# Layer 2's token tiles, normalised and turned inside layer 1's attention

## The chip, the cores and the metric

The kernel runs on one core of a Trainium2 chip. The metric is the device time of one execution in microseconds (us). Names of engines as in the profile: PE is TensorE's matmul, PEld its weight load, DVE is VectorE, ACT is ScalarE, POOL is GpSimd, SP is SyncE, which issues most DMAs.

## What is computed

The reference is a backbone of two layers over 1024 latent tokens and 256 context tokens of width 1024, all in float32. Each layer adds a gated mixer of a normalised input to its tokens:

```python
for i in range(DEPTH):
    ...
    hx = rms_norm(x, norm_g[i]) * (1.0 + scale_x[:, None]) + shift_x[:, None]
    hc = rms_norm(ctx, norm_g[i]) * (1.0 + scale_c) + shift_c
    if kind == 0:
        yx, yc = window_gqa(hx, hc, a_w_in[j], a_sink[j], a_w_out[j], cos_a, sin_a, need_ctx)
    elif kind == 1:
        yx, yc = latent_attention(hx, hc, b_w_in[j], b_q_norm[j], b_w_uq[j], b_kv_norm[j],
                                  b_w_ukv[j], b_w_out[j], cos_b, sin_b, need_ctx)
    ...
    x = x + gate_x[:, None] * yx
```

Layer 1 is a windowed attention with grouped heads and a sink, layer 2 an attention over a latent projection (kv of 256 columns and 32 rotary ones, q of 512, a gate of 1024). The change stands where one layer hands its tokens to the next: rms_norm and the affine map with scale and shift, which give h, and the first projections of h.

## The kernel before

The tokens are ten tiles of 128: tiles 0 and 1 are context, 2 to 9 latent. Two tiles are a pair; h is kept by pairs. All matmuls of the projections are made of three: each operand is split into a rounded part and a rest (`split`: a cast on ACT, L121, and a subtraction on DVE or POOL, L122), and `mm3` issues the three products (L126 to L128).

The order of the work is that in which the program issues it, rearranged by a scheduler within each engine; every engine then runs its own list in order and waits on others by semaphores. On-chip memory is two arenas, F (float32) and R (rounded halves), in which buffers are named by an offset in KB per partition; a `Ring` hands out buffers in turn, and what is written over earlier contents waits until these have been read.

*Layer 1's attention* walks over 40 units: ten tiles in the order 2, 0, 3, 1, 4 to 9, with four groups of heads each. A unit scores four heads (L586) and takes the minimum and the mask on DVE (L597), the exponential on ACT (L600), turns the probabilities by chunks of 128 keys (L617, then the cast L121 and the subtraction L122) and multiplies them with V (L627). The steps of neighbouring units are interleaved: a unit's scores are issued two units ahead, its gate (`g_d`) two, its q three. At a unit's end `fin` copies the product (L637) and adds its halves (L639); `fin2`, one unit later, turns the reciprocal sums, copies them (L648), and makes the gated output. After the fourth group of a tile its output projection is handed out in pieces among the next tile's units (`outproj`, L657 to 676): the tile's x is loaded (L658), the product with the gate vector is taken on DVE (L674), added (L675), and the result is stored to the DRAM buffer `x1_d` (L676).

*The start of layer 2* loads each tile back from `x1_d` (`norm_x`, L212), takes its sum of squares on ACT (L214), the mean and the power of -1/2 (L215 on DVE, L216 on POOL), scales the tile on DVE (L217), turns it with eight transposes in two banks (`turn_x`, L224), and copies them (L225) into the turned pair of `[8, 256]`. `build_h` then applies scale and shift by eighths (L238 on DVE), casts (L241 on ACT) and subtracts (L243, here on DVE). Pairs 0 and 1 are made ahead of the last pieces of the last output projection, pairs 2 to 4 inside the loop over the ten kv tiles. A kv tile is 24 matmuls of 288 columns (`kv_tile`); its statistic (L958 to 960) scales it (L997 on DVE), and two tiles later its turn stands on PE (L1010). The weights of layer 2 come through a ring of staging buffers `stg`: loaded by L264, cast on ACT and subtracted on DVE (the kv block) or POOL (the others). The vector q_norm is loaded by ACT's queue (L972) to F at 8 KB, where layer 1's gate vector `gx` lay, and multiplied on DVE (L973).

## Time and profile before

| | before |
|---|---|
| median of three runs | 1597.75 us (1595.53, 1597.75, 1597.89) |
| the profiled execution | 1596.15 us |
| its span, first to last instruction | 1594.4 us |
| mean granted TensorE clock | 0.997 of full speed |
| PE, PEld busy | 98%, 77% |
| DVE, ACT, POOL busy | 57%, 49%, 47% |
| DMA | 192.82 MB, mean 121 GB/s |

The profile is one execution. A row of a group names line, engine and operation, what it writes and reads, and how often; then busy time, the mean of one in ns, the idle time of the engine just ahead of it, and what ended that. A row of a timeline gives start and length in us; brackets hold the idle time ahead. A stretch is start and end in us. An engine's idle time costs nothing where another engine sets the pace.

### The profile page before, as it was taken

The page shows a single profiled execution, that of the slowest core. Times are in us where ns is not written, and L with a number is a line of the kernel's source. Part 1 is how long each engine was busy: PE and PEld are TensorE (multiplying, and loading weights), DVE is VectorE, ACT ScalarE, POOL GpSimd, SP SyncE. Part 2 cuts the span into 40 slices and gives each one's busy share as a digit, 9 for nine tenths or more (in the row PEclk, how much of TensorE's full clock was granted, in tenths as well). Part 3 has the DMA queues.
Part 4 walks back from the last instruction along what each step waited for, and adds up shares of the span by engine and source line. Part 5 has one row for each costly group of instructions (what it writes and reads, how often), then busy time and mean ns, then how long its engine had stood idle before and what let it go on. Part 6 is the DMA issues. An engine that isn't in the chain of part 4 may idle for free.

```text
span 1594.4 us, 26916 instructions
## 1 busy us (share of the span) xinstructions
PE 1555.2 (98%) x9938; PEld 1222.6 (77%) x9938; DVE 905.9 (57%) x1629; ACT 777.0 (49%) x1478; POOL 742.1 (47%) x805
## 2 busy tenths in 40 slices
PE   7899999999999999998999999999999999999998
PEld 4787777887878888887998899766766766766687
DVE  3515551618777777768525302667677677667454
ACT  3522232348777777767523332455545555555322
POOL 1231112115664444454113350388688688689510
PEclk9999999999999999999999999999999999999999
DMA  7446776354333333327113753313232233244251
GB/s 253 166 138 196 233 210 190 97 153 120 109 110 94 97 93 94 93 79 244 35 34 106 262 184 94 103 30 101 69 96 80 76 88 96 67 130 118 67 167 66
DMA packets 147203, 192.82 MB, mean 121 GB/s; under 512 B 13936, under 2 KB 84080, under 8 KB 147072
## 3 DMA queue, kind: packets, MB, share of 16 engines
q1 hardware_dynamic: 145456, 188.94, 39.5%
q10 hardware_dynamic: 1616, 2.17, 0.5%
q8 instruction: 78, 1.28, 0.4%
q14 instruction: 53, 0.43, 0.1%
HBM read 144.90 MB, written 46.15 MB: 120 GB/s over the span
## 4 chain that ended last, share of the span: by engine, by line
PE 86%; issue 2%; DVE 2%; POOL 2%; ACT 2%; DMA 1%; SPq 0%; POOLq 0%; DVEq 0%; ACTq 0%
PE PB L126 15%; PE PB L127 14%; PE PB L128 14%; PE PB L1303 11%; PE PB L1325 8%; PE PB L586 5%; PE PB L627 4%; PE PB L1266 4%; PE PB L617 4%; PE PB L183 1%; PE PB L1274 1%; PE PB L1354 1%; PE PB L646 1%; ACT arena_r L121 1%; DVE arena_r L122 1%
## 5 line engine op out<-in xcount | busy, mean ns | idle before, releaser
L126 PE MATMUL PB<-arena_r 128*128 128x512 f32 (+3 forms) x1496 | 509.9, 342 | 4.9 <-POOL arena_r L653 2.0
L127 PE MATMUL PB<-arena_r 128*128 128x512 f32 (+3 forms) x1496 | 502.4, 336 | 4.2 <-DVE arena_r L390 2.1
L128 PE MATMUL PB<-arena_r 128*128 128x512 f32 (+3 forms) x1496 | 500.3, 335 | 0.3 <-DVE arena_r L122 0.3
L1317 POOL TENSOR_TENSOR arena_f<-arena_f 128x512 f32<-128x512 f32 x252 | 328.3, 1303 | 82.1 <-ACT arena_f L1309 65.3
L126 PEld LDWEIGHTS PB<-arena_r 128*128 128x128 f32 x1496 | 283.7, 190 | 52.7 <-issue 12.5
L127 PEld LDWEIGHTS PB<-arena_r 128*128 128x128 f32 x1496 | 284.5, 190 | 32.0 <-DVE arena_r L390 3.5
L128 PEld LDWEIGHTS PB<-arena_r 128*128 128x128 f32 x1496 | 284.5, 190 | 28.3 <-DVE arena_r L122 0.5
L122 POOL TENSOR_TENSOR arena_r<-arena_f,arena_r 128x512 fp32r<-128x512 f32 x88 | 115.2, 1325 | 299.7 <-ACT arena_r L121 255.5
L1309 ACT ACTIVATE arena_f<-PB 128x1024 f32<-128x1024 f32 x160 | 164.1, 1027 | 108.9 <-PE PB L1303 65.9
L1268 DVE TENSOR_REDUCE arena_f<-PB 128x1 f32<-128x1024 f32 x128 | 156.1, 1219 | 86.7 <-PE PB L1266 86.6
L1303 PE MATMUL PB<-arena_r 64*128 64x512 f32 (+1 forms) x1600 | 202.3, 392 | 0.3 <-ACT arena_f L1309 0.3
L1303 PEld LDWEIGHTS PB<-arena_r 64*128 64x128 f32 (+1 forms) x1600 | 146.1, 185 | 31.5 <-ACT arena_f L1309 1.8
L122 DVE TENSOR_TENSOR arena_r<-PB,arena_r 128x512 fp32r<-128x512 f32 (+1 forms) x186 | 124.2, 674 | 61.9 <-ACT arena_r L121 61.0
L1325 PE MATMUL PB<-arena_f 128*64 128x512 f32 x640 | 144.4, 597 | 0.0
L600 ACT ACTIVATE arena_f<-arena_f,small 128x640 f32<-128x640 f32 (+2 forms) x160 | 119.5, 747 | 35.4 <-DVE small L597 32.7
L597 DVE CUSTOM_DVE_ANT_0 arena_f<-PB,arena_f,small 128x640 f32<-128x640 f32 (+2 forms) x176 | 125.2, 722 | 20.1 <-PE PB L586 12.6
L121 ACT CAST arena_r<-PB 128x512 fp32r<-128x512 f32 (+1 forms) x186 | 105.3, 573 | 47.4 <-PE PB L617 45.2
L121 ACT CAST arena_r<-arena_f 128x512 fp32r<-128x512 f32 (+3 forms) x141 | 83.8, 603 | 86.7 <-PE PB L128 12.5
L627 PE MATMUL PB<-arena_r 128*128 128x512 f32 x336 | 115.8, 429 | 0.5 <-DVE arena_f L639 0.5
L586 PE MATMUL PB<-arena_r 128*128 128x256 f32 (+1 forms) x576 | 111.0, 308 | 1.6 <-DVE small L597 1.3
L1325 PEld LDWEIGHTS PB<-arena_f 128*64 128x64 f32 x640 | 43.1, 136 | 83.2 <-issue 79.9
L617 PE MATMUL PB<-ident,arena_f 128*128 128x128 f32 x672 | 104.2, 274 | 1.3 <-DVE arena_r L122 0.8
(177 smaller groups left out, 1842.9 us busy)
## 6 DMA issues: line engine op xcount, KB each, us to landing
arena_f<-ada_w SPq DMA_DIRECT2D x47, 512.0 KB, 5.4
arena_r<-q_d SPq DMA_DIRECT2D x80, 256.0 KB, 3.9
arena_r<-qn_d SPq DMA_DIRECT2D x64, 256.0 KB, 3.9
arena_r<-qr_d SPq DMA_DIRECT2D x192, 64.0 KB, 3.3
arena_f<-a_w_in SPq DMA_DIRECT2D x40, 256.0 KB, 3.6
arena_f<-x SPq DMA_DIRECT2D x16, 512.0 KB, 6.6
g_d<-arena_f SPq DMA_DIRECT2D x32, 256.0 KB, 2.1
q_d<-arena_f SPq DMA_DIRECT2D x64, 128.0 KB, 2.4
```

What stands on the lines that cost most here:

```text
L121: nc.scalar.copy(hi, src)
L122: (lo_eng or nc.vector).tensor_sub(lo, src, hi.bitcast(F32))
L126: nc.tensor.matmul(o, ah, bh, start=first, stop=False)
L127: nc.tensor.matmul(o, al, bh, start=False, stop=False)
L128: nc.tensor.matmul(o, ah, bl, start=False, stop=last)
L586: nc.tensor.matmul(S[:, at : at + n], qT[:, s, hq, :], kT[:, g, k : k + n], start=s == 0, stop=s == 1)
L617: nc.tensor.transpose(pt[:, h, :], self.Ps[h][:, ci * 128 : ci * 128 + 128], ident)
L627: nc.tensor.matmul(self.pv, V[:, self.chunks[ci], self.g, :], PT[:, s], start=ci == 0 and s == 0, stop=ci == self.m - 1 and s == 1,)
L1303: nc.tensor.matmul(S[:, t], k[r, c : c + 128], q[r], start=j == 0, stop=j == 4)
L1309: nc.scalar.activation(E, self.S, AF.Exp)
L1317: eng.tensor_add(self.acc, self.acc, E[:, t])
L1325: nc.tensor.matmul(self.pv[p : p + 64], Vq[:, cs[t], self.h % 4, :], E[:, t], start=i == 0, stop=i == 4)
```

## The change

`norm_x` is parted into the load and `scale_x`. A DRAM buffer `xT_d` holds four turned pairs. The generator `pre_turns` does, for tiles 0 to 7: load the tile from `x1_d` into the one buffer `xpre`; scale it (L219 to 222: the lines of `scale_x` in the changed kernel); turn one half of it into a bank of the attention's own two (L689), copy that on ACT (L690) into the one buffer `tpre`, and store it to `xT_d` (L692); the same for the other half. These four steps are called at the ends of the attention's units, from tile position 5 on, two for each unit (one at position 8). At unit 38 pair 0 is loaded from `xT_d`, two halves of 256 KB.

Layer 2 loads pairs 1, 2 and 3 (`load_xt`) in place of `build_x`; `build_h` works on two half buffers. h(2) and h(3) are built at kv tiles 0 and 2. Tiles 8 and 9 are normalised and turned in layer 2 as before, and h(4) is built at kv tile 5. The buffers of F are laid out anew: `or1`, `rtr`, `gr`, `junk`, `stg` (three of 512 words for three of 576), `xr` (two for three), the last three of `qst`; `xtr` goes. The instructions on PE, DVE, ACT and POOL are as many as before; SP issues 24 DMAs more.

```diff
@@ -74,6 +74,7 @@
     q0_d = dpool.tile([4, 64, 2, NT, 512], F32, name="q0_d")
     g0_d = dpool.tile([8, 128, TOK], F32, name="g0_d")
     x1_d = dpool.tile([TOK, D], F32, name="x1_d")
+    xT_d = dpool.tile([4, 128, 8, 256], F32, name="xT_d")
     qn_d = dpool.tile([8, 128, 2, SEQ], F32, name="qn_d")
     qr_d = dpool.tile([4, 128, 2, SEQ], F32, name="qr_d")
     g1_d = dpool.tile([8, 128, SEQ], F32, name="g1_d")
@@ -210,37 +211,35 @@
     def norm_x(src, xr, junk):
         x = xr.next()
         load(out=x, in_=src)
+        scale_x(x, junk)
+        return x
+
+    def scale_x(x, junk):
         st = sm_ring()
         nc.scalar.activation(junk, x, AF.Square, accum_out=st[:, 0:1])
         nc.vector.tensor_scalar(st[:, 1:2], st[:, 0:1], 1.0 / D, EPS, ALU.mult, ALU.add)
         nc.gpsimd.tensor_tensor(st[:, 2:3], st[:, 1:2], mhalf, ALU.pow)
         nc.vector.tensor_scalar_mul(x, x, st[:, 2:3])
-        return x
 
     def turn_x(x, xt, j):
         for q in range(2):
             ps = shp(pst(), 4, 128)
             for c in range(4):
                 nc.tensor.transpose(ps[:, c, :], x[:, (4 * q + c) * 128 : (4 * q + c + 1) * 128], ident)
-            nc.scalar.copy(xt[:, 4 * q : 4 * q + 4, j * 128 : j * 128 + 128], ps)
-
-    def build_x(p, src, xr, xtr, junk):
-
-        xt = shp(xtr.next(), 8, 256)
-        for j in range(2):
-            turn_x(norm_x(src(2 * p + j), xr, junk), xt, j)
-        return xt
+            nc.scalar.copy(xt[q][:, :, j * 128 : j * 128 + 128], ps)
 
     def build_h(p, xt, hT, A, B, fast=False, ks=range(8)):
 
         w = 1 if p == 0 else 0
         for k in ks:
-            nc.vector.tensor_scalar(xt[:, k, :], xt[:, k, :], A[:, k, w : w + 1], B[:, k, w : w + 1], ALU.mult, ALU.add)
+            x = xt[k // 4][:, k % 4, :]
+            nc.vector.tensor_scalar(x, x, A[:, k, w : w + 1], B[:, k, w : w + 1], ALU.mult, ALU.add)
             if k % 2:
+                x = xt[k // 4][:, k % 4 - 1 : k % 4 + 1, :]
                 hi = hT[:, 0, k - 1 : k + 1, :]
-                nc.scalar.copy(hi, xt[:, k - 1 : k + 1, :])
+                nc.scalar.copy(hi, x)
                 eng = nc.vector if fast or k % 4 == 1 else nc.gpsimd
-                eng.tensor_sub(hT[:, 1, k - 1 : k + 1, :], xt[:, k - 1 : k + 1, :], hi.bitcast(F32))
+                eng.tensor_sub(hT[:, 1, k - 1 : k + 1, :], x, hi.bitcast(F32))
 
     class SmallRing:
         def __init__(self, n, w):
@@ -515,9 +514,9 @@
     ytmp = Ring(F, [12], 512)
     wstg = Ring(F, [4, 6, 12], 512)
     rbr = Ring(F, [42, 47], 256)
-    or1, rtr = (Ring(F, [o, o - 5], 256) for o in (43, 45))
+    or1, rtr = Ring(F, [43, 44], 256), Ring(F, [45, 41], 256)
     Pr = Ring(F, [14 + 2.5 * i for i in range(8)], 640)
-    gr = Ring(F, [2.5, 34, 46], 256)
+    gr = Ring(F, [34, 35, 46], 256)
     xr0 = Ring(F, [4], 1024)
     Wo = [r_at(o, 2, 1024) for o in (16, 24, 32, 40, 48, 56, 0, 8)]
     ogr = Ring(R, [64, 72], 2048)
@@ -676,6 +675,34 @@
         load(out=x1_d[ti * 128 : ti * 128 + 128, :], in_=x)
 
     units = [UnitA(ti, g) for ti in ORDER for g in range(4)]
+    xpre, tpre = f_at(48, 1024), f_at(36, 4, 128)
+
+    def pre_turn(ti):
+        load(out=xpre, in_=x1_d[ti * 128 : ti * 128 + 128, :])
+        yield
+        scale_x(xpre, f_at(36, 512).bitcast(BF16))
+        yield
+        for q in range(2):
+            ps = shp(pst3(), 4, 128)
+            for c in range(4):
+                k = 4 * q + c
+                nc.tensor.transpose(ps[:, c, :], xpre[:, k * 128 : k * 128 + 128], ident)
+            nc.scalar.copy(tpre, ps)
+            ts = slice(ti % 2 * 128, ti % 2 * 128 + 128)
+            load(out=xT_d[ti // 2, :, 4 * q : 4 * q + 4, ts], in_=tpre)
+            yield
+
+    def pre_turns():
+        for ti in range(8):
+            yield from pre_turn(ti)
+
+    xt_at = [[f_at(o, 4, 256) for o in os] for os in ((48, 36), (14, 18), (22, 26), (14, 18), (22, 26))]
+
+    def load_xt(p):
+        for q in range(2):
+            load(out=xt_at[p][q], in_=xT_d[p, :, 4 * q : 4 * q + 4, :])
+
+    pre = pre_turns()
 
 
     def wo_load():
@@ -910,6 +937,10 @@
             while i > 0 and done < -(-8 * i // steps):
                 next(filler, None)
                 done += 1
+        for _ in range({5: 2, 6: 2, 7: 2, 8: 1, 9: 2}.get(ui // 4, 0)):
+            next(pre, None)
+        if ui == 38:
+            load_xt(0)
         u.fin(og)
         fins.append(u.fin2)
         if u.g == 3:
@@ -930,10 +961,9 @@
     sinb = f_at(1, 8, 32)
     qn = f_at(8, 512)
     kvn = f_at(10, 256)
-    junk = f_at(34.5, 512).bitcast(BF16)
-    stg = Ring(F, [30, 32.25, 49.5], 576)
-    xr = Ring(F, [22, 26, 45], 1024)
-    xtr = Ring(F, [14, 37], 2048)
+    junk = f_at(40, 512).bitcast(BF16)
+    stg = Ring(F, [30, 32, 44], 512)
+    xr = Ring(F, [48, 36], 1024)
     ev = Ring(F, [2, 4, 6, 12], 512)
     ukK = r_at(134, 2, 2, 1024)
     ukV = r_at(64, 2, 2, 1024)
@@ -961,10 +991,10 @@
         return st[:, 2:3]
 
     fetch1(0, nc.vector)
-    xts = {0: build_x(0, src1, xr, xtr, junk)}
-    build_h(0, xts.pop(0), hT1[0], ada1.A, ada1.B, fast=True)
-    xts[1] = build_x(1, src1, xr, xtr, junk)
-    build_h(1, xts.pop(1), hT1[1], ada1.A, ada1.B, fast=True)
+    load_xt(1)
+    build_h(0, xt_at[0], hT1[0], ada1.A, ada1.B, fast=True)
+    load_xt(2)
+    build_h(1, xt_at[1], hT1[1], ada1.A, ada1.B, fast=True)
     load2(out=cosb, in_=t["cos_b"].rearrange("p (t d) -> p t d", t=8))
     load2(out=sinb, in_=t["sin_b"].rearrange("p (t d) -> p t d", t=8))
     for _ in last_outproj:
@@ -1097,17 +1127,17 @@
         ch = (c0 - 800) // 128
         load(out=g1_d[ch : ch + 2, :, (p - 1) * 256 : p * 256].rearrange("c p n -> p c n"), in_=shp(gg, 2, 256))
 
-    nx = norm_x(src1(4), xr, junk)
+    load_xt(3)
+    nx = {8: norm_x(src1(8), xr, junk)}
     for ti in range(NT):
-        n = ti + 3
-        if 4 <= n < NT:
-            if n % 2 == 0:
-                xt = shp(xtr.next(), 8, 256)
-            turn_x(nx, xt, n % 2)
-            if n + 1 < NT:
-                nx = norm_x(src1(n + 1), xr, junk)
-            if n % 2:
-                build_h(n // 2, xt, hT1[n // 2], ada1.A, ada1.B, fast=True)
+        if ti in (0, 2):
+            build_h(ti // 2 + 2, xt_at[ti // 2 + 2], hT1[ti // 2 + 2], ada1.A, ada1.B, fast=True)
+        if ti == 1:
+            nx[9] = norm_x(src1(9), xr, junk)
+        if ti in (4, 5):
+            turn_x(nx[ti + 4], xt_at[4], ti % 2)
+        if ti == 5:
+            build_h(4, xt_at[4], hT1[4], ada1.A, ada1.B, fast=True)
         kv_tile(ti)
         flush(2)
         if ti > 1 and ti % 2:
@@ -1119,7 +1149,7 @@
     fetch1(3, nc.vector)
     fetch1(4)
     rtmp = Ring(F, [14, 28], 512)
-    qst = Ring(F, [16, 20, 24, 37, 41, 45], 1024)
+    qst = Ring(F, [16, 20, 24, 36, 48, 8], 1024)
     for ti in range(8):
         qr_tile(ti)
         flush(2)
```

On ACT, around the first pre-turned tile in the attention (position 5 of ten). L600, L637, L648 and L121 of before are L599, L636, L647 and L122 of the changed kernel. Before:

```order
L637 COPY arena_f<-PB 64x256 x2
L121 CAST arena_r<-PB 128x512
L600 ACTIVATE arena_f,small<-arena_f,small 128x640
L648 COPY arena_f<-PB 128x256
L121 CAST arena_r<-PB 128x512
L600 ACTIVATE arena_f,small<-arena_f,small 128x640 x2
L121 CAST arena_r<-PB 128x512
```

and now:

```order
L636 COPY arena_f<-PB 64x256 x2
L690 COPY arena_f<-PB 128x512
L599 ACTIVATE arena_f,small<-arena_f,small 128x640
L647 COPY arena_f<-PB 128x256
L122 CAST arena_r<-PB 128x512
L599 ACTIVATE arena_f,small<-arena_f,small 128x640 x2
L690 COPY arena_f<-PB 128x512
L122 CAST arena_r<-PB 128x512
```

The two copies of the tile's halves (L690) have come in among the unit's exponentials and casts; the second stands five instructions behind the first, and of the casts that stood between the copies of the product (L637) and the third exponential one stands later now.

On DVE, from the last product of the last output projection to the first scaled kv tile. In before L674 and L675 are the product and the addition, L217 scales a tile of x, L238 and L243 build h, L973 scales q_norm, L959 belongs to kv's statistic and L997 is the scaled kv tile:

```order
L674 TENSOR_TENSOR arena_f<-PB,arena_f 128x512
L217 TENSOR_SCALAR arena_f<-arena_f,small 128x1024
L238 TENSOR_SCALAR arena_f<-arena_f,small 128x256 x6
L243 TENSOR_TENSOR arena_r<-arena_f,arena_r 128x512 x3
L238 TENSOR_SCALAR arena_f<-arena_f,small 128x256 x2
L675 TENSOR_TENSOR arena_f<-arena_f 128x512
L973 TENSOR_SCALAR arena_f<-arena_f 128x512
L959 TENSOR_SCALAR small<-small 128x1
L243 TENSOR_TENSOR arena_r<-arena_f,arena_r 128x512
L997 SCALAR_TENSOR_TENSOR arena_f<-PB,small,arena_f 128x256
```

and now (L673, L674, L236, L242, L1003, L989 and L1027 are the same steps):

```order
L673 TENSOR_TENSOR arena_f<-PB,arena_f 128x512
L1003 TENSOR_SCALAR arena_f<-arena_f 128x512
L674 TENSOR_TENSOR arena_f<-arena_f 128x512
L236 TENSOR_SCALAR arena_f<-arena_f,small 128x256 x5
L242 TENSOR_TENSOR arena_r<-arena_f,arena_r 128x512 x3
L236 TENSOR_SCALAR arena_f<-arena_f,small 128x256 x2
L989 TENSOR_SCALAR small<-small 128x1
L236 TENSOR_SCALAR arena_f<-arena_f,small 128x256
L1027 SCALAR_TENSOR_TENSOR arena_f<-PB,small,arena_f 128x256
```

The scaling of q_norm stood behind the building of a pair and stands now directly behind the last product; the pair built there is pair 1 in before and pair 2 now. On PE the first kv turn (L1010 in before, L1040 now) stands behind 75 matmuls of 288 columns.

## The prediction

> **What bounds the kernel now.** I read the page first, then the table of stretches, then what TensorE waited for at the end of the first attention. The page's busy line and the head of its chain:
>
> ```profile
> PE 1555.2 (98%) x9938; PEld 1222.6 (77%) x9938; DVE 905.9 (57%) x1629; ACT 777.0 (49%) x1478; POOL 742.1 (47%) x805
> PE 86%; issue 2%; DVE 2%; POOL 2%; ACT 2%; DMA 1%; SPq 0%; POOLq 0%; DVEq 0%; ACTq 0%
> ```
>
> TensorE is busy for 98% of the span and is most of the chain, so an edit pays only where TensorE idles or runs at a lower clock. The stretches (start:end, length, then busy time of PE, PEld, DVE, ACT, POOL, then the granted clock, the DMA share and GB/s) tell the attention apart from the start of layer 2:
>
> ```profile
> 480.00:700.00 220.00, 219.40 (x1318) 188.57 (x1317) 168.01 (x341) 161.44 (x378) 111.92 (x193) 1.00 0.32 94
> 720.00:762.00 42.00, 34.24 (x224) 30.60 (x223) 36.25 (x79) 30.96 (x66) 18.73 (x21) 0.96 0.69 212
> 750.00:754.00 4.00, 4.00 (x35) 4.00 (x33) 3.51 (x4) 1.91 (x5) 4.00 (x5) 1.00 0.54 150
> 754.00:758.00 4.00, 0.91 (x8) 0.71 (x6) 4.00 (x9) 2.97 (x6) 0.99 (x1) 0.96 0.64 180
> 758.00:762.00 4.00, 3.77 (x21) 3.78 (x22) 3.66 (x12) 3.04 (x9) 1.62 (x3) 0.61 0.00 0
> ```
>
> The attention (480 to 700 us) is full: 0.6 us of 220 idle. ACT and DVE are at 73% and 76% there, POOL at 51%. The start of layer 2 (720 to 762) has 42.00 - 34.24 = 7.8 us of idle TensorE, and its clock falls behind the longest hole: 4 x 0.04 + 4 x 0.39 = 1.7 us lost in the last two stretches. Together 9.5 us: that is all the change can win. The waits behind it, from 700 to 860 us (line <- releaser: us, times, longest):
>
> ```profile
> PE PB L1010 <- ACT arena_f L225: 3.3, 1, 3.3
> PE PB L224 <- DVE small L959: 1.2, 1, 1.2
> PE PB L126 <- ACT arena_r L241: 1.1, 1, 1.1
> PE PB L224 <- DVE arena_f L217: 0.9, 1, 0.9
> PE PB L127 <- DVE arena_r L243: 0.6, 1, 0.6
> PE PB L224 <- DVE small L215: 0.5, 1, 0.5
> PE PB L128 <- DVE arena_r L122: 0.3, 1, 0.3
> PE PB L627 <- DVE arena_f L639: 0.2, 1, 0.2
> ```
>
> Three waits of the turns (L224, 2.6 us) and two for the halves of h (1.7 us) belong directly to the step that is moved. The largest, 3.3 us at L1010, turns a kv result; what it has to wait for is everything queued on DVE and ACT ahead of that result.
>
> **The change part by part.** *The turns.* These are the rows of what eight of ten tiles move (the counts are those of ten tiles):
>
> ```profile
> L224 PE MATMUL PB<-ident,arena_f 128*128 128x128 f32 x80 | 11.2, 276 | 2.8 <-DVE small L959 1.2 <-DVE arena_f L217 0.9 <-DVE small L215 0.5
> L225 ACT COPY arena_f<-PB 128x512 f32<-128x512 f32 x20 | 11.2, 585 | 2.4 <-PE PB L224 2.4
> L214 ACT ACTIVATE arena_f<-arena_f 128x1024 bf16<-128x1024 f32 x10 | 10.6, 1059 | 0.7 <-DMA arena_f<-x_d 0.5
> L214 ACT ACTIVATION_READ_ACCUMULATOR arena_f<-arena_f 128x1 f32 x10 | 1.9, 190 | 0.0
> L217 DVE TENSOR_SCALAR arena_f<-arena_f,small 128x1024 f32<-128x1024 f32 x10 | 7.5, 753 | 4.5 <-POOL small L216 4.4
> L216 POOL TENSOR_TENSOR small<-small 128x1 f32<-128x1 f32 x10 | 6.0, 602 | 10.1 <-DVE small L215 9.2 <-DVE small L959 0.8
> ```
>
> On TensorE the 64 transposes cost the same in both places. Eight of them take from one start to the next matmul:
>
> ```profile
> 748.52 1.09 PE L224 MATMUL PB<-ident,arena_f 128*128 128x128 f32 x8 [1.24 <-DVE small L959]
> 749.36 0.38 PE L126 MATMUL PB<-arena_r 128*128 128x288 f32 x1
> ```
>
> 0.84 us, so 8 x 0.84 = 6.7 us leave layer 2 and 6.7 us come into an attention that has no hole for them: net nothing. What counts is idle time alone.
>
> *What the attention pays.* ACT gets 8 x (1.059 + 0.190 + 2 x 0.585) = 19 us, DVE 8 x 0.753 = 6 us plus small ones, POOL 8 x 0.602 = 5 us. In the 180 us in which they fall, ACT and DVE have idle a quarter of the time (some 48 and 43 us), so there is room on average. The cost is order: every engine works in order, and a copy that waits holds the casts behind it, for which P x V on TensorE waits. The one new wait of that kind is the single buffer of the turned half: the second copy (L690 after) waits until the store of the first half has been read out. Between the two copies ACT has one exp, one copy of 128x256, one cast and two exps, by these rows (from 500 to 600 us; L617 are the attention's own turns that the cast follows):
>
> ```profile
> L600 ACT ACTIVATE arena_f<-arena_f,small 128x640 f32<-128x640 f32 x40 | 33.4, 834 | 7.9 <-DVE small L597 6.9
> L121 ACT CAST arena_r<-PB 128x512 fp32r<-128x512 f32 x49 | 28.5, 586 | 18.4 <-PE PB L617 18.1
> L617 PE MATMUL PB<-ident,arena_f 128*128 128x128 f32 x200 | 29.6, 272 | 0.0
> L648 ACT COPY arena_f<-PB 128x256 f32<-128x256 f32 x10 | 3.6, 356 | 0.0
> g_d<-arena_f SPq DMA_DIRECT2D x32, 256.0 KB, 2.1
> x_d<-arena_f SPq DMA_DIRECT2D x6, 512.0 KB, 2.7
> arena_f<-x SPq DMA_DIRECT2D x5, 512.0 KB, 3.5
> ```
>
> Cover: 3 x 0.834 + 0.356 + 0.586 = 3.4 us. The store moves 256 KB; the nearest row is g_d's 2.1 us, a 512 KB store takes 2.7. With some 0.4 us until SP has issued it, the round trip is 2.5 to 3.1 us: under the cover, with 0.3 to 0.9 us in hand. If a 512 KB load is ahead of it in the DMA queue (3.5 us), the round trip is up to about 4.7 and ACT stands 1.3 us. The 1.25 us Square and the two copies also delay a cast by up to their own length, against the idle of 18.1 us in 49 casts that ACT has in waiting for L617, 0.37 us each. So per tile 0 to 0.75 us of TensorE, all in 0 to 6 us; not below nothing by more than the 0.6 us that the stretch idles now. I take 1.7 us, 0.2 for each tile, since the row that is nearest (the g_d store) leaves the cover standing and no TensorE wait over 0.2 us stands in this stretch now. What SP issues more (8 loads and 16 stores, and loads of the turned pairs for two of x1) goes at nothing: loads of q and g are issued three and two units ahead, and the DMA share is 0.32. If a store waits on SP for its copy, those loads are what is queued behind it.
>
> The DVE scale of 753 ns also meets POOL there. In layer 2 a DVE scale of this kind beside POOL's subtractions has this spread (ns, min/median/max):
>
> ```profile
> L238 DVE TENSOR_SCALAR arena_f<-arena_f,small x40: 402/414/1390, 725.2 to 782.9; 128x256 f32<-128x256 f32 x40
> ```
>
> The longest is 0.98 us over the median. At half the tiles (POOL is busy half the time) that is 4 us of DVE, inside its 43 us of idle, and in the 0 to 6 above. The Trainium skill, "SBUF — State Buffer", section "Who interferes with whom", has a rule that speaks against the move: a tensor_scalar in a two-port mode and GpSimd exclude each other, and the later one is blocked for the whole instruction of the other. The spread of L238 agrees with it; by the rule alone a scale could wait a whole POOL instruction for each tile, which would be 8 waits on DVE instead of my 4.
>
> *What layer 2 gets.* The normalising of pairs 0 to 3 leaves it; h(0) and h(1) are built from loaded halves before the last output projection ends, as the order shows, so kv tiles 0 to 2 follow the attention directly. TensorE then runs 75 matmuls of 288 columns before the first kv turn (now L1040). Their pitch, from these two, nine steps apart:
>
> ```profile
> 745.79 0.29 PE L128 MATMUL PB<-arena_r 128*128 128x288 f32 x1
> 746.98 0.29 PE L128 MATMUL PB<-arena_r 128*128 128x288 f32 x1
> ```
>
> 1.19 / 9 = 0.132 us, so TensorE reaches L1040 9.9 us after it starts on kv. What L1040 needs is the scaled kv result (L1027 on DVE). In DVE's new order the scaling of q_norm (L1003) stands right behind the last product of the attention's output, and waits for a load that may not start before that product, because q_norm lands where the gate lay. Behind it stand an addition, eight scales, three subtractions of h(2) and the statistic:
>
> ```profile
> 732.81 4.28 DMA arena_f<-b_q_norm
> L243 DVE TENSOR_TENSOR arena_r<-arena_f,arena_r 128x512 fp32r<-128x512 f32 x20 | 13.3, 705 | 0.6 <-ACT arena_r L241 0.6
> 751.16 5.60 DVE L238 TENSOR_SCALAR arena_f<-arena_f,small 128x256 f32<-128x256 f32 x8
> 750.94 4.05 POOL L122 TENSOR_TENSOR arena_r<-arena_f,arena_r 128x512 fp32r<-128x512 f32 x3
> ```
>
> Product 0.7, load 4.3 and 0.4 until issued, L1003 0.4, addition 0.7, eight scales 8 x 0.414 = 3.3 when undisturbed and 5.6 beside POOL's subtractions (the last two rows), 3 x 0.705 = 2.1, statistic, power (0.6, as L216's) and L1027 together about 1.5, an estimate: 13.4 to 15.7 us, against 9.9. So L1040 waits 3.5 to 5.8 us; the square of that statistic on ACT also stands behind the cast of the fourth piece of a weight block whose staging buffer POOL must free first (another 1 us, an estimate), and if the load is issued ahead of its place it is 2. I take 5, from 2 to 7. A hole of 3.3 us was followed by the half clock that cost 1.7 us; I put the same 1.7 behind this one. The Trainium skill, "TensorE: Matmul & The Clock Gate", section "Part 1: The HAM clock gate", has the clock fall to a half after an idle window of about 3.4 us whose phase runs free of the kernel; the trace agrees (0.61 behind 3.31 us of idle), and by that rule the drop could stay away at a hole of 5 us only where none of its windows lies idle.
>
> Beside it I estimate a wait of 0.4 us for kv's first operands (the ones for halves of h are 0.6 and 1.1 now) and 0 to 1.5 for the second kv turn, say 0.3. New loss 5 + 1.7 + 0.4 + 0.3 = 7.4 us, for 9.5 now: a gain of 2.1 us (at the ends: 9.5 - 2.4 = 7.1, and 9.5 - 10.7 = -1.2). The turned pairs' loads must land ahead of h(0); the first is issued two units before the attention ends, and I charge it nothing. Were it late, kv would start up to 2.5 us later.
>
> **Sum.** 1.7 - 2.1 = -0.4 us. The profiled execution took 1596.15 us (span 1594.4), 1.6 us under the median of the three runs, 1597.75. From the median: 1597.3 us. About 0.2% (3.2 us) is what a measurement of this kernel can tell from no change.
>
> **The rivals.** *The hole goes (faster).* If q_norm's load lands early enough, or the builds run undisturbed and ACT's statistic is not held, L1027 is done within 10 us and L1040 waits under 1 us; the clock stays full. Then 9.5 falls to about 1 us and, with 1.7 paid in the attention, the time is 1597.75 - 8.5 + 1.7 = 1591.0. For it: ten tiles' work on DVE and ACT there shrinks to little; against it: the 4.28 us load, which the order puts in front of everything on DVE.
>
> *ACT stands at the store (slower).* The second copy of each tile waits for the store of the first, and the casts of the attention stand behind it. It decides from a round trip of 3.4 us on. At 4.7 us each of eight tiles loses 1.3 us: 10.4 - 2.1 = +8.3, 1606.0. For it: a 512 KB load of the next tile and of the output projection pass in the same queues, and TensorE has no slack; against it: the 2.1 and 2.7 us of the stores now, and a DMA share of 0.32.
>
> *The change moves nothing that counts.* The turns' own waits are 2.6 us; if only they go and 1.7 is paid, the time is 1597.75 - 2.6 + 1.7 = 1596.9. This is near my forecast, and part of its share.
>
> **How the numbers follow.** Forecast (a hole like the one before, a full attention): 0.58, and of it 0.12 lies beyond 3.2 us on the fast side and 0.05 on the slow one. Hole gone: 0.24, faster. ACT at the store: 0.18, slower. Faster 0.12 + 0.24 = 0.36, slower 0.05 + 0.18 = 0.23, same 0.41. The forecast's own range is -5.4 (1.7 - 7.1) to +4.8 (6 - 1.2): 1592.3 to 1602.5. The range for 8 in 10 reaches to 1590.5, past the rival's 1591.0, and to 1603.5, into the smaller stalls of the other.
>
> **What would show it.** Right: from 480 to 720 us TensorE idles 1 to 3 us; L1040 waits some 5 us, with DVE's L1003 waiting for b_q_norm ahead of it, and the clock falls behind it. Wrong: TensorE waits on L690 or on L122 again and again in the attention (the slower rival), or no wait over 1 us stands at L1040 and the clock stays at 1.00 (the faster one).

## The result, and the profile after

The changed kernel takes 1623.11 us (median of five runs, 1620.21 to 1624.31); before takes 1597.89 us. The ratio is 1.0149, with a 95% interval of 1.0138 to 1.0161: slower by 24 us by that ratio and by 25.2 by the two medians, where the prediction had 1597.3 and a range that ended at 1603.5. The profiled execution has a span of 1621.5 us, 27.1 more than before.

The page of the changed kernel, the lines that answer to the first two shown of before:

```profile
PE 1566.3 (97%) x9938; PEld 1229.6 (76%) x9938; DVE 895.8 (55%) x1629; ACT 778.0 (48%) x1478; POOL 746.4 (46%) x805
PE 80%; DMA 5%; DVE 4%; issue 4%; POOL 3%; ACT 3%; SPq 1%; ACTq 0%; POOLq 0%; DVEq 0%
```

TensorE runs the same 9938 matmuls and is busy 11 us longer; the clock that is lost, counted below (7.2 + 5.0 us, 1.6 before), accounts for 10.6 of them. And 5% of the chain are DMAs, which were 1%. The stretches from the attention's middle up to the first kv matmul at 757 us (columns as before):

```profile
480.00:540.00 60.00, 59.68 (x357) 51.51 (x356) 46.59 (x95) 45.07 (x104) 32.18 (x57) 1.00 0.37 112
540.00:600.00 60.00, 54.16 (x305) 46.15 (x303) 38.81 (x79) 39.21 (x88) 24.52 (x41) 0.91 0.37 104
600.00:660.00 60.00, 53.30 (x311) 44.81 (x310) 37.95 (x77) 40.42 (x92) 24.69 (x43) 0.97 0.42 122
660.00:720.00 60.00, 58.59 (x359) 50.09 (x359) 45.70 (x96) 46.10 (x108) 31.38 (x53) 1.00 0.42 128
720.00:757.00 37.00, 35.35 (x191) 28.97 (x191) 29.60 (x66) 23.21 (x52) 14.61 (x23) 1.00 0.54 174
```

The attention is full until 540 us and then is not: 277 - 261.1 = 15.9 us of idle TensorE, and 60 x 0.09 + 60 x 0.03 = some 7.2 us lost to the clock (it is given to two digits), 23.1 in all. Before, from 480 us to its first kv matmul at 730, TensorE was idle for 1.4 us of 250 at full clock. So this place alone has lost 21.7 us more. What TensorE waits for from 480 to 745 us:

```profile
PE PB L616 <- ACT arena_f L690: 12.6, 7, 3.1
PE PB L626 <- DVE arena_f L638: 1.9, 5, 0.4
PE PB L626 <- ACT arena_f L599: 0.6, 1, 0.6
```

These are 15.1 of the 15.9 us. It is the slower rival's wait: the attention's own turns (L616) stand for a bank that the second copy of a tile's half (L690) has not emptied. And that copy waits for the store (the group, 535 to 745 us):

```profile
L690 ACT COPY arena_f<-PB 128x512 f32<-128x512 f32 x16 | 9.4, 587 | 13.7 <-DMA xT_d<-arena_f 12.9 <-PE PB L689 0.6
```

One tile in time, from SP's, ACT's and TensorE's timelines. On SP the next tile's 512 KB load goes out just ahead of the first store:

```profile
545.04 0.33 SPq L681 DMA_DIRECT2D arena_f<-x_d  x1
545.46 0.39 SPq L692 DMA_DIRECT2D xT_d<-arena_f  x1
547.62 1.16 SPq L561 DMA_DIRECT2D arena_r<-q_d  x2
```

On ACT the last exponential ahead of the copy has ended at 549.42 us; then the copy:

```profile
551.48 0.59 ACT L690 COPY arena_f<-PB 128x512 f32<-128x512 f32 x1 [2.06 <-DMA xT_d<-arena_f]
```

TensorE after it, with two matmuls of the same form further on:

```profile
552.12 0.98 PE L616 MATMUL PB<-ident,arena_f 128*128 128x128 f32 x4 [2.04 <-ACT arena_f L690]
...
555.68 0.62 PE L616 MATMUL PB<-ident,arena_f 128*128 128x128 f32 x4
```

From the store's issue to the copy's start it takes 551.48 - 545.46 = 6.0 us, the longest of the seven that ACT waits for (3.1 to 6.0). From the first copy's end, as the prediction counted, it is 6.5 us (3.7 to 6.5); the prediction put 2.5 to 3.1 there, 4.7 at the worst. Four turns take 0.98 us behind the hole and 0.62 a few us on. The stretches around it:

```profile
550.00:552.00 2.00, 0.08 (x1) 0.00 (x0) 0.00 (x0) 0.52 (x2) 0.00 (x0) 1.00 0.80 210
552.00:554.00 2.00, 1.88 (x9) 1.88 (x10) 0.93 (x2) 1.25 (x4) 1.18 (x2) 0.57 0.49 148
554.00:556.00 2.00, 2.00 (x8) 1.50 (x7) 1.26 (x3) 0.00 (x0) 0.43 (x2) 0.57 0.00 0
```

This hole of 2 us costs another 1.7 us in clock (4 x 0.43); from 556 us on the clock is full again.

Layer 2, from the first kv matmul to the last (757 to 825 us; before 730 to 798, equally long):

```profile
757.00:768.00 11.00, 9.79 (x69) 9.09 (x68) 8.28 (x17) 4.51 (x10) 1.65 (x2) 1.00 0.77 231
768.00:772.00 4.00, 1.24 (x10) 1.01 (x8) 4.00 (x6) 1.95 (x5) 2.93 (x3) 1.00 0.68 215
772.00:776.00 4.00, 0.00 (x0) 0.00 (x0) 3.55 (x8) 2.08 (x6) 2.34 (x2) 0.77 0.52 158
776.00:780.00 4.00, 3.83 (x16) 3.83 (x17) 4.00 (x6) 2.03 (x4) 3.84 (x3) 0.50 0.67 238
780.00:784.00 4.00, 4.00 (x30) 4.00 (x30) 4.00 (x10) 2.64 (x5) 0.61 (x2) 0.88 0.51 137
784.00:788.00 4.00, 1.80 (x16) 1.59 (x14) 3.22 (x8) 1.89 (x8) 2.69 (x3) 0.98 0.25 68
788.00:825.00 37.00, 36.70 (x280) 36.46 (x281) 13.47 (x54) 13.28 (x31) 5.59 (x14) 0.96 0.07 22
```

Idle 68 - 57.4 = 10.6 us and some 5.0 us of clock. In before the same stretch had 68 - 60.8 = 7.2 us idle and 1.6 us of clock. In before the turns of the later pairs fall into it, and it is no shorter now that most of them are gone. The first kv turn is what waits, from TensorE's timeline:

```profile
776.17 0.69 PE L1040 MATMUL PB<-ident,arena_f 128*128 128x128 f32 x2 [6.93 <-DVE arena_f L1027]
...
787.95 0.69 PE L1040 MATMUL PB<-ident,arena_f 128*128 128x128 f32 x2 [2.20 <-DVE arena_f L1027]
```

and DVE's queue ahead of the first of them:

```profile
765.87 0.43 DVE L1003 TENSOR_SCALAR arena_f<-arena_f 128x512 f32<-128x512 f32 x1 [2.66 <-DMA arena_f<-b_q_norm]
766.22 0.68 DVE L674 TENSOR_TENSOR arena_f<-arena_f 128x512 f32<-128x512 f32 x1
766.82 4.58 DVE L236 TENSOR_SCALAR arena_f<-arena_f,small 128x256 f32<-128x256 f32 x5
771.32 1.88 DVE L242 TENSOR_TENSOR arena_r<-arena_f,arena_r 128x512 fp32r<-128x512 f32 x3
773.13 1.67 DVE L236 TENSOR_SCALAR arena_f<-arena_f,small 128x256 f32<-128x256 f32 x2
774.72 0.14 DVE L989 TENSOR_SCALAR small<-small 128x1 f32<-128x1 f32 x1
774.79 0.40 DVE L236 TENSOR_SCALAR arena_f<-arena_f,small 128x256 f32<-128x256 f32 x1
775.64 0.48 DVE L1027 SCALAR_TENSOR_TENSOR arena_f<-PB,small,arena_f 128x256 f32<-128x256 f32 x1 [0.45 <-POOL small L990]
```

The order that the prediction read is there, step by step. Five scales take 4.58 us beside POOL's subtractions, where 5 x 0.414 = 2.1 would do.

The account: 21.7 us more lost before the first kv matmul, 15.6 - 8.8 = 6.8 more behind it, 28.5 for 27.1 of span; ahead of 480 us the changed kernel idles 2.0 us less. From layer 2's first exponential to the end both kernels take the same 577.7 us (1016.7 to 1594.4, 1043.8 to 1621.5).

### The profile page after: what moved, and what is told of

The parts are those of the page before. It is cut to its first block, busy times and chain, and to the rows that moved or that the text cites. A ratio compares the mean times of both kernels' runs of the same rounds, so it can differ in the third digit from the quotient of the medians.

```text
span 1621.5 us, 26907 instructions
## 1 busy us (share of the span) xinstructions
PE 1566.3 (97%) x9938; PEld 1229.6 (76%) x9938; DVE 895.8 (55%) x1629; ACT 778.0 (48%) x1478; POOL 746.4 (46%) x805
## 3 DMA queue, kind: packets, MB, share of 16 engines
q10 hardware_dynamic: 1616, 2.17, 0.5%
## 4 chain that ended last, share of the span: by engine, by line
PE 80%; DMA 5%; DVE 4%; issue 4%; POOL 3%; ACT 3%; SPq 1%; ACTq 0%; POOLq 0%; DVEq 0%
PE PB L127 13%; PE PB L128 13%; PE PB L129 13%; PE PB L1333 11%; PE PB L1355 8%; PE PB L1296 4%; PE PB L585 3%; PE PB L616 3%; PE PB L626 3%; DMA xT_d<-arena_f 2%; PE PB L184 2%; PE PB L1304 1%; PE PB L1384 1%; ACT arena_r L122 1%; DVE arena_r L123 1%
## 5 line engine op out<-in xcount | busy, mean ns | idle before, releaser
L1347 POOL TENSOR_TENSOR arena_f<-arena_f 128x512 f32<-128x512 f32 x252 | 324.8, 1289 | 79.2 <-ACT arena_f L1339 62.4
L599 ACT ACTIVATE arena_f<-arena_f,small 128x640 f32<-128x640 f32 (+2 forms) x160 | 119.4, 747 | 36.1 <-DVE small L596 34.1
L122 ACT CAST arena_r<-arena_f 128x512 fp32r<-128x512 f32 (+3 forms) x141 | 84.0, 603 | 92.3 <-DMA arena_f<-b_w_in 15.9
L122 ACT CAST arena_r<-PB 128x512 fp32r<-128x512 f32 (+1 forms) x186 | 105.4, 573 | 46.8 <-PE PB L616 40.8
L616 PE MATMUL PB<-ident,arena_f 128*128 128x128 f32 x672 | 107.8, 278 | 13.9 <-ACT arena_f L690 12.6
L585 PE MATMUL PB<-arena_r 128*128 128x256 f32 (+1 forms) x576 | 114.4, 314 | 1.6 <-DVE small L596 1.3
L616 PEld LDWEIGHTS PB<-ident,arena_f 128*128 128x128 f32 x672 | 83.2, 142 | 33.3 <-ACT arena_f L690 15.3
```

Of the source, the lines that this page charges most:

```text
L122: nc.scalar.copy(hi, src)
L585: nc.tensor.matmul(S[:, at : at + n], qT[:, s, hq, :], kT[:, g, k : k + n], start=s == 0, stop=s == 1)
L616: nc.tensor.transpose(pt[:, h, :], self.Ps[h][:, ci * 128 : ci * 128 + 128], ident)
L1347: eng.tensor_add(self.acc, self.acc, E[:, t])
```

## The experiments

Theory A: ACT runs in order and stands for DMA round trips that the turned tiles have brought into the attention; what is behind it are the casts for P x V. Its rival B: the work that the turns bring to the engines, and their banks. For layer 2, theory C (DVE's queue ahead of the first scaled kv tile) stands against D (ACT's casts and POOL's subtractions of weights ahead of its statistic). "Attention" below is the time from the first unit's product copies to the last's: 346.4 us before (370.3 to 716.7), 377.6 in the changed kernel (369.6 to 747.2), of which the prediction's 6.7 us are the transposes themselves.

| run | time, us | ratio to before, 95% interval | attention, us |
|---|---|---|---|
| changed kernel | 1623.11 | 1.0138 to 1.0161 | 377.6 |
| two buffers | 1623.34 | 1.0151 to 1.0183 | 378.3 |
| long rows | 1619.59 | 1.0126 to 1.0157 | 372.6 |
| store by ACT | 1639.18 | 1.0244 to 1.0278 | 392.6 |
| no loads | 1608.52 | 1.0055 to 1.0085 | 365.5 |
| no stores | 1614.35 | 1.0083 to 1.0117 | 370.2 |
| neither | 1607.68 | 1.0047 to 1.0085 | 360.8 |
| three buffers | 1621.25 | 1.0123 to 1.0167 | 374.8 |
| tied Square, first run | 1605.68 | 1.0037 to 1.0066 | 358.8 |
| tied Square, loads one unit later | 1604.47 | 1.0022 to 1.0048 | 359.9 |
| late h(2), changed attention | 1623.35 | 1.0150 to 1.0181 | 378.6 |
| tied Square, late h(2) | 1602.17 | 1.0016 to 1.0038 | 358.3 |
| and the casts tied | 1603.85 | 1.0020 to 1.0046 | 358.2 |

**Two buffers.** The first copy's buffer is no longer the second's:

```diff
-    xpre, tpre = f_at(48, 1024), f_at(36, 4, 128)
+    xpre, tprer = f_at(48, 1024), Ring(F, [36, 38], 512)
...
+            tpre = shp(tprer.next(), 4, 128)
             nc.scalar.copy(tpre, ps)
```

> The turned halves alternate between two buffers (F at 36 and 38 KB), so the second copy no longer waits for the first store. Theory A (ACT stands 12.9 us in all for the store, and each hole also halves the clock behind it): both go, TensorE's waits on L690 fall from 12.6 us to under 1, the clock from 540 to 740 us is 1.00, the time falls by about 20 us to 1603. Theory B (the Square, the copies and the banks that the turns take are what costs): the waits move to other lines and the time stays over 1612.

The waits on the copy are gone, as theory A had it; but the time has not moved and the waits stand at other lines, which is what theory B had. What TensorE waits for there now (480 to 745 us):

```profile
PE PB L585 <- DVE small L596: 8.0, 3, 3.0
PE PB L616 <- DVE arena_r L123: 4.6, 4, 2.0
```

and what ACT waits for (535 to 740 us):

```profile
ACT arena_f L219 <- DMA arena_f<-x_d: 7.1, 4, 2.5
ACT arena_f L219 <- DMA xT_d<-arena_f: 5.6, 3, 2.4
```

The Square (L219) has taken over, and not where it stood. In the changed kernel, from ACT's timeline, tile 1's Square comes up 12.6 us behind its load (issued at 545.04) and waits for nothing; with two buffers it comes up 4.7 us behind it (issued at 547.89):

```profile
557.64 1.04 ACT L219 ACTIVATE arena_f<-arena_f 128x1024 bf16<-128x1024 f32 x1
554.36 1.06 ACT L219 ACTIVATE arena_f<-arena_f 128x1024 bf16<-128x1024 f32 x1 [1.82 <-DMA xT_d<-arena_f]
```

With the store's wait gone from the program, the scheduler has put the Square ahead of casts that stood before it. For tiles 1 to 5 it comes up 4.2 to 4.7 us behind its load, where it was 10.6 to 12.6. There it waits for the load; and it writes its useless output to F at 36 KB, which is the first turned half, so that it waits for that half's store as well. DVE then stands in its own order for the Square's sum (L220, 18.9 us; 0.6 in the changed kernel), and through DVE TensorE. The edit took one wait away, and the new order of ACT brought another.

**Why the store takes 6 us.** Two runs with one buffer:

```diff
-    xT_d = dpool.tile([4, 128, 8, 256], F32, name="xT_d")
+    xT_d = dpool.tile([8, 128, 8, 128], F32, name="xT_d")
...
-            load(out=xT_d[ti // 2, :, 4 * q : 4 * q + 4, ts], in_=tpre)
+            load(out=xT_d[ti, :, 4 * q : 4 * q + 4, :], in_=tpre)
```

> One buffer as in the changed kernel; only the layout of xT_d differs, so that a store writes rows of 2 KB where it wrote rows of 512 B, and the pairs' loads read it in twice as many pieces. Theory A1 (the store is slow for its 512 B rows): the store lands in about 2.5 us, ACT's wait for it falls from 12.9 us to under 3, time about 1606. Theory A2 (the store is slow because it stands behind the 512 KB load of the next tile): the wait stays at 10 to 13 us, time about 1622.

```diff
-            load(out=xT_d[ti // 2, :, 4 * q : 4 * q + 4, ts], in_=tpre)
+            load2(out=xT_d[ti // 2, :, 4 * q : 4 * q + 4, ts], in_=tpre)
```

> One buffer, 512 B rows as in the changed kernel; the store is issued on ACT's queue, not behind the load of the next tile on SP's. Theory A2 (place in SP's queue): the wait falls to under 4 us and the time to about 1608, with some 0.4 us more on ACT for each store. Theory A1 (512 B rows): the wait stays at 10 us or more, time 1618 to 1624.

Long rows bring TensorE's waits on L690 from 12.6 to 11.7 us and the time down by 3.5; the short rows are a small part. A store on ACT's own queue is worse: ACT's wait at the copy is 18.0 us where it was 12.9, and the time is 16 us longer, outside both expectations. Tile 0's store, issued at 546.43 at the same time as the next load (546.44), takes 6.3 us to the copy's start. Place in SP's queue is therefore not what makes the store slow. What is left is what runs beside it.

**Without the loads, without the stores.** Three runs that leave transfers of tiles 1 to 7 out:

```diff
-        load(out=xpre, in_=x1_d[ti * 128 : ti * 128 + 128, :])
+        if ti == 0:
+            load(out=xpre, in_=x1_d[ti * 128 : ti * 128 + 128, :])
```

> Only tile 0 is loaded for the turns; tiles 1 to 7 turn what is left in its buffer, so their 512 KB loads are left out (the output is not the reference's); stores, buffers and engines' work are as in the changed kernel. Theory A (ACT stands in order for DMA round trips; the load of the next tile slows the store): the waits on the second copy fall from 12.6 us to under 5, the attention, 377.6 us from the first to the last unit's copies in the changed kernel and 346.4 before, takes 355 to 364, the time is 1601 to 1610. If the store is slow by itself: the waits stay over 9 us. Theory B (engine work and banks): attention over 370, time over 1616.

```diff
-            load(out=xT_d[ti // 2, :, 4 * q : 4 * q + 4, ts], in_=tpre)
+            if ti == 0:
+                for p in range(4):
+                    for j in range(2):
+                        load(out=xT_d[p, :, 4 * q : 4 * q + 4, 128 * j : 128 * j + 128], in_=tpre)
```

> The loads stay, the stores of the turned halves are left out for tiles 1 to 7 (tile 0's halves are stored in all places, once; the output is not the reference's). Theory A: no wait at the copies; the Square still stands for its tile's load where it comes less than 4 to 6 us behind it; attention 356 to 368, time 1602 to 1614. Theory B: attention over 370, time over 1616.

> Neither the loads nor the stores of tiles 1 to 7 (the output is not the reference's); all work on the engines stays. Theory A: the attention pays the 6.7 us of the moved transposes and little else, 353 to 356 us, its clock is full, the time is 1598 to 1602. Theory B: attention over 365 us, time over 1612.

Without the loads, TensorE's waits at the copy fall from 12.6 to 7.5 us and the attention by 12, the clock's share among it: the holes in the attention are at most 1.75 us now and its clock stays full. The store lands faster with no 512 KB load beside it, but still not under cover. From its issue to the copy it takes 4.0 us at tile 0 (546.22 to 550.24), 3.7 to 4.6 at tiles 0 to 4, where the changed kernel has 4.9 to 6.0. The waits lie between the two expectations; the time is theory A's.

The packets in the traces show where the store's time goes. In the changed kernel, from 545.46 us, the store's issue, to 548.1, only the load's packets of 4096 bytes move; the first of 512 bytes, the size of the store's rows, comes 2.7 us behind the issue, without the loads 0.9 us. At tiles 1, 3 and 5 it is the 512 KB store to x1_d that was issued just ahead, and 1.7 us. The rest has another companion: at tiles 0 to 4, in both runs, a packet of 16 KB of the queue that the profile's page lists as "instruction", 0.9 to 1.8 us long, falls into the store's time. At tile 5 there is none, and the copy starts 3.1 us behind the issue, without the loads 2.6 us and with no wait. These times fit last rows that stand behind such a packet; no run took it away, so that part is not shown.

Without the stores the attention takes 370.2 us and the run 1614.35, which neither theory's numbers fit whole (up to 368 and 1614, over 370 and 1616); the Square now waits 7.1 us for loads, and at tile 0, whose sixteen stores remain, one unit takes 20.0 us where before has 10.1. Without either the attention takes 360.8, again with some 7 us at tile 0 (a unit of 17.0 us where 10.1 was); the rest is near the 353 to 356 expected, and TensorE is idle for only 1.9 us of the 160 from 560 to 720. The time, 1607.68, lies above theory A's 1602 and below theory B's 1612. All the engines' work is still there. So theory B falls for the attention: the work costs little more than its transposes, the transfers cost the rest.

**Three buffers, and the tied Square.** First, though it was run last, only a place of its own for the Square's output:

```diff
-    gr = Ring(F, [34, 35, 46], 256)
+    gr = Ring(F, [2.5, 34, 46], 256)
...
-    xpre, tpre = f_at(48, 1024), f_at(36, 4, 128)
+    xpre, tprer = f_at(48, 1024), Ring(F, [35, 37], 512)
...
-        scale_x(xpre, f_at(36, 512).bitcast(BF16))
+        scale_x(xpre, f_at(39, 512).bitcast(BF16))
```

> Two buffers for the turned halves and one of its own for what the Square writes; the loads and the Square stand where the changed kernel's order puts them. In the run with two buffers alone the Square waited 5.6 us for stores out of the memory that it writes and 7.1 us for its tile's load. Theory A (each of these waits costs by itself): the waits for stores are gone, those for the load, some 7 us, stay; attention 364 to 373 us (378.3 with two buffers, 359.9 with the tied Square), time 1609 to 1617. If only the load counts: no better than with two buffers, 1620 or more. If the shared memory was the whole of it: as with the tied Square, 1604 to 1606.

A miss for theory A's sum. The waits for stores are gone; ACT's wait for DMAs from 535 to 750 us is now this one:

```profile
ACT arena_f L219 <- DMA arena_f<-x_d: 10.8, 6, 2.3
```

The load's share has grown by 3.7 of the 5.6 us that the stores' has lost, and the time, 1621.25, is within 2 us of the changed kernel: the line "if only the load counts" has it. In ACT's order the Square comes up 3.5 to 4.3 us behind its load at tiles 1 to 5 and stands until that lands. Then a kernel in which every tile is loaded a unit ahead and the Square cannot come earlier in ACT's order:

```diff
+            nc.vector.tensor_scalar(st[:, 3:4], after, 0.0, 1.0, ALU.mult, ALU.add)
+            nc.scalar.activation(junk, x, AF.Square, scale=st[:, 3:4], accum_out=st[:, 0:1])
...
+        if nnu:
+            seen[0] = nnu.nm[:, 1:2]
+        for _ in range(pre_at.get(ui, 0)):
```

The factor 1 made from a later unit's minimum ties it. The first run of it:

> A whole kernel again: two buffers for the turned halves, a third for what the Square writes (in the changed kernel that lay in the turned half's memory), each tile loaded one unit ahead of its Square, and the Square tied by a small DVE operation to a later unit's minimum, so that it cannot stand in ACT's order before it. Theory A: ACT waits for no DMA, attention 353 to 358 us, time 1598 to 1604; what is left over before is the start of layer 2. Theory B: attention over 365 us, time over 1612.

It took 1605.68 us with an attention of 358.8, 1.7 and 0.8 us over the range. With the loads put one unit later:

> The kernel with two buffers, a buffer of its own for the Square's output and the tied Square, with every tile's load one unit later than in the run before (that one loaded tile 0 over the context's gate vector, which tile 1 still needed; its time stands for the same work). Theory A: as there, attention 357 to 360 us, time 1604 to 1607. If its time came from the wrong gate: over 1610.

1604.47 us, 18.6 under the changed kernel, and the attention's stretches are full at full clock again:

```profile
540.00:600.00 60.00, 59.39 (x361) 50.77 (x359) 46.82 (x98) 46.73 (x106) 29.73 (x49) 1.00 0.40 117
600.00:660.00 60.00, 59.53 (x363) 51.01 (x362) 45.70 (x97) 45.90 (x107) 31.92 (x53) 1.00 0.49 147
660.00:720.00 60.00, 58.28 (x355) 48.65 (x354) 45.77 (x100) 45.38 (x109) 32.46 (x55) 1.00 0.36 113
```

Idle 2.8 us of 180, where the changed kernel had 13.9 and the lower clock. Work, copies, stores and loads are all there; only where ACT meets them has changed. The Square comes up 11.0 to 14.4 us behind its load, and ACT waits for no transfer of the turned tiles. This settles the attention for theory A. What the tie and the earlier load are worth each was not parted. The first kv matmul now stands at 739.0 us, 8.5 behind before's: 48 more transposes ahead of it (before had 16 there, now 64) make 5.0 of that at 0.84 for eight. What is left to lose lies behind it: 10.8 us of idle TensorE and 6.8 of clock up to the last kv matmul, where before lost 7.2 and 1.6.

**Layer 2.** In the changed kernel's attention, with q_norm's factor taken into the statistic of q, and h(2) and h(3) tied behind the first scaled kv tile:

```diff
-    nc.vector.tensor_scalar_mul(qn, qn, B_SCALE)
...
+        nc.vector.tensor_scalar(st[:, 1:2], st[:, 0:1], 1.0 / (n * s * s), EPS / (s * s), ALU.mult, ALU.add)
...
-        if ti in (0, 2):
-            build_h(ti // 2 + 2, xt_at[ti // 2 + 2], hT1[ti // 2 + 2], ada1.A, ada1.B, fast=True)
+        if ti == 1:
+            A2 = shp(sm(16), 8, 2)
+            nc.vector.scalar_tensor_tensor(A2, kv_e[0][:, 0:16].rearrange("p (k w) -> p k w", k=8), 0.0, ada1.A, ALU.mult, ALU.add)
+            build_h(2, xt_at[2], hT1[2], A2, ada1.B, fast=True)
+        if ti == 2:
+            build_h(3, xt_at[3], hT1[3], A2, ada1.B, fast=True)
```

> The attention as in the changed kernel. In layer 2 the scaling of q_norm on DVE is left out (the factor goes into the statistic of q), and the building of h(2) and h(3) is tied by a small DVE operation to the first scaled kv tile, so that it stands behind it. Theory C (the hole at L1040 is DVE's queue: the wait for q_norm and the building of h(2) ahead of L1027): the waits at L1040 fall from 9.1 us to under 3, the clock there is full, time 1623 less 8 to 10, about 1614. Theory D (the hole is set by ACT's statistic behind the casts of weights, or by the load of kv_norm): the hole stays over 4 us and the time over 1619.

The first hole falls from 6.9 to 2.4 us, the second grows from 2.2 to 5.0, the time stays. TensorE's timeline:

```profile
775.61 0.44 PE L1040 MATMUL PB<-ident,arena_f 128*128 128x128 f32 x2 [2.38 <-DVE arena_f L1026]
...
788.52 0.69 PE L1040 MATMUL PB<-ident,arena_f 128*128 128x128 f32 x2 [5.01 <-DVE arena_f L1026]
```

ACT's, around the statistic of the first tile (L988):

```profile
770.06 1.94 ACT L122 CAST arena_r<-arena_f 128x512 fp32r<-128x512 f32 x3 [4.82 <-DMA arena_f<-b_w_in]
771.91 0.38 ACT L988 ACTIVATE arena_f<-PB 128x256 bf16<-128x256 f32 x1
```

and POOL's, around its power (L990):

```profile
770.76 3.76 POOL L123 TENSOR_TENSOR arena_r<-arena_f,arena_r 128x512 fp32r<-128x512 f32 x3 [5.99 <-DMA arena_f<-b_w_in]
774.48 0.56 POOL L990 TENSOR_TENSOR small<-small 128x1 f32<-128x1 f32 x1
```

DVE was free and waited. The statistic stood behind three casts of a weight block whose load had come late, the power behind their subtractions. Theory C was right on what stood ahead, and D on what comes next and on the time.

The same edit on the kernel with the tied Square, and then with the casts tied too:

> The kernel with the tied Square, and in layer 2 q_norm's scaling left out and h(2), h(3) built behind the first kv tile. Theory C (DVE's queue ahead of L1027 makes the hole at the first kv turn): that hole, 9.6 us in the kernel with the tied Square alone, goes under 2, the time falls by 8 to 12 us to about 1595. Theory D (ACT's casts of the next weight block and POOL's subtractions stand ahead of the statistic as well): a hole of 2 to 5 us stays at the first kv turn, another comes at the second, the time falls by 1 to 5 us, to 1601 to 1605.

```diff
-    fetch1(6)
-    fetch1(1)
...
+            one = sm(1)
+            nc.vector.tensor_scalar(one, kv_e[0][:, 0:1], 0.0, 1.0, ALU.mult, ALU.add)
+            fetch1(6, None, one)
+            fetch1(1, None, one)
...
+            nc.scalar.activation(hi, src, AF.Copy, scale=gate_hi)
```

> As the last, and the casts of the gate's first weight block and of q's first are tied behind the first kv tile too, so that neither they nor their subtractions stand ahead of its statistic and power. Theory D: both holes at the kv turns go under 2 us and the clock stays full, time 1593 to 1598. Theory E (what is short there is data: the weights come later now, and PE waits for them instead): a wait of 4 us or more at matmuls that read the new weights, time 1602 or more.

The first kv turn waits 8.5 us with the tied Square alone (its L1051), 4.9 with late h(2), 3.2 with the casts tied; in the last, from TensorE's timeline, the weights are late as well (this profiled execution, 1599.96 us, is the fastest of the ten):

```profile
755.72 0.38 PE L130 MATMUL PB<-arena_r 128*128 128x256 f32 x1 [1.22 <-ACT arena_r L125]
757.98 0.58 PE L131 MATMUL PB<-arena_r 128*128 128x256 f32 x1 [1.87 <-POOL arena_r L126]
763.94 0.69 PE L1052 MATMUL PB<-ident,arena_f 128*128 128x128 f32 x2 [3.25 <-DVE arena_f L1038]
```

1604.47, 1602.17 and 1603.85 us: the intervals of neighbours overlap, so neither of the two last steps is told from none for certain. For the first of them theory D had the size (1 to 5 us less were expected, 2.3 measured) and the hole that stays, but no hole over 1 us came at the second kv turn. For the second neither fits whole: D's holes under 2 us did not come, and E's time did, with 3.1 us at the new weights where it had 4. None of the kernels beats the one before. That layer 2's start is held by its data, weights and turned pairs that are loaded at the same time, is what these rows point to; no run tests it by itself.

## Why the prediction was wrong

The direction of risk was seen, its weight was not. Point by point:

- *The transposes cost the same in both places.* Right in the main: with the tied Square two neighbouring units of the attention, one tile's worth, take 21.3 us (10.4 and 10.9) for 20.1 before, 1.2 a tile against 0.84 of transposes, so 0.4 a tile is not accounted for.
- *The store's round trip of 2.5 to 3.1 us stays under a cover of 3.4.* This is the step that failed. Counted from the first copy's end, it took 6.5 us at tile 0 and 5.5 to 6.1 at the next four. The row it was taken from, g_d's 2.1, is a median, and of stores that all stand outside this stretch (113 to 361 us, and from 764 on); the first 24 of them alone spread from 2.0 to 6.7 us where their landing is on record. This store stood behind a 512 KB transfer in each of the tiles 0 to 5, the next tile's load or the store to x1_d. Without the loads it is 4.0 us at tile 0. The prediction's worst case, 4.7, was still too short, though it had named the load. The cover was read at the first tile and is not the same for all: without the wait the second copy would have come 4.4 us behind the first's end at tiles 0, 2 and 4, but 2.6 at tiles 1, 3 and 5, where one exponential less stands between them.
- *What SP issues more goes at nothing.* This term failed with it: without the loads of tiles 1 to 7 the time is 14.6 us less.
- *0.2 us for each tile, 1.7 in all, 6 at the most.* 21.7 us were lost: 12.6 of waits on the second copy, some 2 of smaller ones, and the clock behind three of the holes (7.2 us), which the prediction charged in layer 2 and not in the attention. The Square, taken as 1.25 us of work, was no more than that in the changed kernel, at tiles 1 to 5 10.6 to 12.6 us behind its load; it became a wait when the scheduler moved it up in the runs with more buffers.
- *The slower rival.* Its mechanism and its place came out: ACT stood 12.9 us at the copies, where it had 10.4. It gave 1606, because it counted the wait and not the clock behind it, and because it kept the gain in layer 2. It had been given a chance of 0.18.
- *L1040 waits 5 us, 2 to 7, clock 1.7, new loss 7.4 us.* The mechanism was right, down to the order; the sizes were not. The wait was 6.9 us at the first kv turn and 2.2 at the second, the clock 5.0, the whole stretch 15.6 us. The load of q_norm did not wait for the last product (762.53 us), as the prediction had it; it was issued at 759.66, behind the one at 758.26, and took 6.2 us for 4.3, beside loads of weights and of turned pairs (their halves are 512 KB each, not the 256 KB given in The change). The scales beside POOL came near their worst, 4.58 us for five. The upper end of this sum, 7 + 1.7 + 0.4 + 1.5, is 10.6 and not 10.7, which changes nothing.
- *A gain of 2.1 us in layer 2.* A loss of 6.8 came. A reading that fits the late casts and weights in the runs on layer 2, but was not tested: the turns that left had filled TensorE while weights were loaded, cast and subtracted, and with them gone the kv tiles stand earlier against the same loads.

## What to carry to other kernels

A step moved into a full stretch is paid in waits, and on an engine that runs in order: list each transfer that the step's instructions wait for, on every engine that they pass, with the landing time that such a transfer has beside the others then running, not the one it has alone. If one such wait is taken away, read the new order before expecting anything: a scheduler that is free to move the next instruction that waits may put it right behind its own load. Here taking the store's wait away moved the time by 2 us at most, and by 18.6 once the Square was tied and its load put earlier as well. Memory that holds nothing of worth, such as a Square's unused output, still makes a wait if it lies where a store is read from.

## What the runs showed of the hardware

The clock fell behind shorter holes than I had expected from before's 3.3 us. In the changed kernel's attention four turns took 0.66 us behind holes of 1.50 and 1.69 us and 0.98 to 1.12 behind 2.04, 2.76 and 3.06. But the length alone does not decide. With two buffers a hole of 1.99 us left the clock full, with three buffers one of 1.99 was followed by a granted clock of 0.57 over four us, without the stores already one of 1.85 (0.66 from 558 to 562 us). Long rows have a hole of 3.09 us that left it full, four turns still in 0.66 us, the store by ACT one of 3.14:

```profile
625.77 0.66 PE L616 MATMUL PB<-ident,arena_f 128*128 128x128 f32 x4 [3.09 <-ACT arena_f L690]
```

So between 1.85 and 3.1 us of idle TensorE both were seen. What a fall costs varies too: 0.79 over the eight us from 552 is 1.7 us lost, 0.57 over the eight from 576, behind 3.06 us, is 3.4. The Trainium skill, "TensorE: Matmul & The Clock Gate", section "Part 1: The HAM clock gate", has the half clock come after at least one idle window of about 3.4 us; the falls behind 1.85 to 2.8 us of idle do not agree, and the measurement decides. Its other half, that the full clock comes back after at least one busy window of about 3.4 us, agrees: 0.57 over the four us from 552 to 556 is 3.4 us at half speed, and 0.57 over the eight from 576 is 6.9.
